# Norms that start earlier and other mixers in finer steps, in a hybrid decoder trunk

## The chip, the cores and the metric

The kernel runs on one core of a Trainium2 chip. The metric is the time of one execution on the device in microseconds (us); less is better. The engines of the core work side by side and wait for each other through semaphores: TensorE (PE) multiplies matrices, VectorE (DVE) and ScalarE (ACT) do elementwise work, GpSimd (POOL) does elementwise work that reads and writes SBUF alone, SyncE (SP) issues transfers; ACT issues transfers too. Each engine takes its own instructions in one fixed order.

## The reference, cut to what matters

```python
def rmsnorm(x, g):
    return x * lax.rsqrt(jnp.mean(x * x, axis=-1, keepdims=True) + 1e-6) * g
def run_layer(x, ...):                       # one layer, D_MODEL 1024
    z = rmsnorm(x, norm1_g) @ w_in           # (positions, 1024) @ (1024, 2432)
    zau, zav, zbu, zcx, zcb, zcc, zd = split(z)
    ya = chunk_gmlp(zau, zav, ...)           # A
    yb = s5_ssm(zbu, ...)                    # B: diagonal complex state space
    yc = short_conv(zcx, zcb, zcc, ...)      # C: y = zb * conv3(zc * zx)
    yd = rwkv7(zd, ...)                      # D: matrix state along the positions
    x = x + concat(ya, yb, yc, yd) @ w_out
    gate, up = split(rmsnorm(x, norm2_g) @ ffn_w_gu)
    return x + (silu(gate) * up) @ ffn_w_down     # FFN, inner width 2816
y_prompt = rmsnorm(run_layer(x_prompt, ...), norm_f_g)   # 2048 positions
y_sample = rmsnorm(run_layer(x_sample, ...), norm_f_g)   # 8 sequences, one position each
```

## The kernel before

The prompt is cut into four pieces of 512 positions (q = 0 to 3); activations lie transposed, features on partitions, positions in columns. The 8 sample columns ride with piece 1 in the mixers (520 columns) and with the last piece in the FFN. Every large product is made of an fp32r pass of the high parts (L281) and two bf16 passes with the low parts (L286), all in `mmg`. A weight tile is loaded into `raw` (three buffers in `wpool`), cast by ACT into `wh` (L240); the low part `wl` is made by DVE (L244) the first time and loaded back from memory (`lod`) afterwards.

The order of the work: first the 17 tiles `z` of piece 0 with the D mixer of that piece (until about 144 us); then `park(q)` for pieces 1, 2 and 3, which computes their z, scales it and puts it to memory (`zdr`), while the other mixers of piece 0 run; then for each piece the output projection (`outphase`), `norm2` and the FFN, beside which the mixers of the next piece run from the parked z; `final` is the last norm. On PE the order is written out: a `Strand` is a generator that yields numbers of ticks, a tick standing for one pass of 512 columns, and strands are taken up between the large products when their ticks have passed. The other engines take the order that the scheduler gives by priority (`hp`).

A norm is a `squares` and an `Rms`. `squares` squares the eight tiles of x (ACT), adds the first ones on POOL (L313) and the last ones on DVE (L317, L319); `rms` sums over partitions on PE (L338), takes a root and one Newton step (`newton`, on POOL unless it is given `V`, that is DVE; its last line is L296), spreads the result on PE (L354) and copies it out (ACT, L358). The gain g is put on x where x is converted to its high part `rh` (ACT) and low part `rl` (DVE, L384). So the products of a tile of z can run before the norm is known; the factor comes with the eviction (`zload` L790 for piece 0, `put_z` L757 for the others). In `norm1` x lies in tiles of the pool `zt_` (six) and the squares in tiles of `raw`:

```python
        def sq():
            return wpool.tile([P, TW], F32, tag="raw", bufs=3, name=nm("sq"))
        return h, Rms(squares(xk, w, sq, True), w, prio=MP, wait=64, gap=48)
```

`zrest` is the start of the mixers A to C: it loads z again, spreads two tiles into U5 (32 small copies, half on ACT, half on DVE, L834), makes the convolution (L850 to L866) and the statistics of v. POOL inverts small triangular matrices for the D mixer (L1259, L1261) and works off the constants of mixer B (`s5Q`, L520), of which ACT stores two halves (`s_q`, L676). In the FFN, L1445 to L1451 make silu(gate) * up (`gp`, `gr`, `ft`, `ah`, `al`) and L1464 adds the down projection into `xm`.

Of the kernel before, what the change touches and what calls it, by code (L numbers as in the profile page):

```python
# [65 lines left out]
def trunk(ctx: ExitStack, tc: tile.TileContext, I, O):  # L66
# [116 lines left out]
    def zwidth(q):  # L183
        return TW if q == SM else TP
# [117 lines left out]
    def squares(xk, w, new=at_, fast=False):  # L302
# [3 lines left out]
        for k in range(KT):  # L306
            if k == 0:
                act(acc[:, :w], xk(k), AF.Square)
                continue
            sq = new()  # L310
            act(sq[:, :w], xk(k), AF.Square)
            if not fast or k < 5:
                G.tensor_tensor(acc[:, :w], acc[:, :w], sq[:, :w], op=ALU.add)  # L313
            elif late is None:
                late = sq
            else:
                V.tensor_tensor(late[:, :w], late[:, :w], sq[:, :w], op=ALU.add)  # L317
# [85 lines left out]
    def norm1(q):  # L403

        w = zwidth(q)
        h = ring_tile(1)

        def xk(k):
            t = zt_("x")
            nc.sync.dma_start(t[:, :w], I["xq"][q, :, k, :w])  # L410
            put_gain(h, k, w, t[:, :w], "n1")
            return t[:, :w]

        def sq():
            return wpool.tile([P, TW], F32, tag="raw", bufs=3, name=nm("sq"))

        return h, Rms(squares(xk, w, sq, True), w, prio=MP, wait=64, gap=48)

# [3 lines left out]

    first = Rms(acc0, TP, wait=60, prio=18000)
    rs0 = acc0

# [80 lines left out]
    def s5_setup():  # L506
        with ExitStack() as c2:
# [183 lines left out]
            for pr in range(8):  # L691
# [4 lines left out]
                for g in range(2):  # L696
                    ps_ = slice(64 * g, 64 * g + 64)
                    for ri in range(2):
# [4 lines left out]
                        else:  # L703
                            act(cv[ps_, ri, g], bc[ps_, 3, pr], AF.Copy, scale=-1.0)
                            act(fv[ps_, ri, :, g], Ft[ps_, 1, pr], AF.Copy, scale=-1.0)
                yield 40 if pr == 0 else 20
                yield from ms_free()
# [76 lines left out]
    def zload(h, m, q, off=0):  # L784
        t = zt_()
        if q in parked:
            nc.sync.dma_start(t[:, off : off + zwidth(q)], zdr[q - 1, m, :, : zwidth(q)])
            return t
        for p_, (c0, n) in zip(ahead0.pop(0) if ahead0 else ztile(h, m, q), zblocks(q)):
            V.tensor_tensor(t[:, off + c0 : off + c0 + n], p_[:, :n], rs0[:, c0 : c0 + n], op=ALU.mult)  # L790
        return t

    def zrw(h, q):
        w = zwidth(q)
        zs = rw.tile([P, 7, TP], F32, tag="zs", name=nm("zs"))
        if q == 0:
            ahead0.extend(ztile(h, m, q) for m in range(4))
            first.done()
# [24 lines left out]
    def zrest(h, q, take):  # L823
# [4 lines left out]
        for j in range(2):  # L828
            zt = zload(h, 7 + j, q)
            for pr in range(4):  # L830
                src = zt[32 * pr : 32 * pr + 32, :TP].rearrange("p (c s) -> p c s", s=4)
                for s in range(4):
                    e = (S.copy, V.tensor_copy)[s % 2]
# [11 lines left out]
        ys = []  # L845
        for j in range(2):
            zx = zload(h, 9 + j, q)
            zz = zload(h, 11 + j, q, 2)
# [8 lines left out]
            if q == SM:  # L857
# [5 lines left out]
                nc.scalar.dma_start(O["cvs"][:, j, 0], cbuf[:, j, 1])  # L863
                nc.scalar.dma_start(O["cvs"][:, j, 1], zq)
            zb = zload(h, 13 + j, q)
            E.tensor_tensor(y[:, :w], y[:, :w], zb[:, :w], op=ALU.mult)  # L866
# [6 lines left out]
        vn = []  # L873
        for g, (b0, nb, rows) in enumerate(groups(q)):
            vt = zt_() if rows == P else vs
            n = 256 * nb
# [532 lines left out]
    def norm2(xm, q):  # L1409
# [7 lines left out]

        return h2, Rms(squares(xk, w, at_, True), w, V, prio=2 * RP, wait=30)

# [80 lines left out]
    def final(xm, q):  # L1500
# [8 lines left out]
        for k, t in enumerate(ts):  # L1509
            act(t[:, :w], xk(k), AF.Copy, scale=col("nf", k))  # L1510
        n = Rms(acc, w, prio=2 * RP, wait=40)

# [112 lines left out]
    m = Mix(0, h)  # L1625
    m.columns()
    m.start()
    with hp(MP):
        m.gm2 = m.rest()
        next(m.gm2)  # L1630
    for q in range(1, npiece):
        with hp(2 * RP):
            h, n1 = norm1(q)
        if q == 1:
# [4 lines left out]
    for q in range(npiece):  # L1639
        nx = Mix(q + 1) if q < last else None  # L1640
        if nx:
            nx.columns()
            nx.start(10)
        with hp(2 * RP):
# [144 lines left out]
```

## Time and profile before

| | |
|---|---|
| time, median of 3 runs | 2643.06 us (2640.42 to 2652.55) |
| the profiled execution's own time | 2647.65 us |
| its span in the profile | 2645.9 us |
| mean granted TensorE clock | 0.955 of full speed |
| busy: PE, DVE, ACT, POOL | 92%, 53%, 40%, 30% |

The profile is of one execution. Its span reaches from the first to the last instruction, its own time is 1.75 us longer. An engine's busy time is the time in which it had an instruction under way. The granted clock is given as a share of full speed (2.4 GHz); the lower of its two levels is 1.2 GHz.

### The profile page before, as it was taken

What the parts mean: (1) busy time and instruction counts of PE and PEld (TensorE: products, weight loads), DVE (VectorE), ACT (ScalarE), POOL (GpSimd) and SP (SyncE); (2) the same over time, 40 slices, a digit from 0 to 9 for tenths busy, and PEclk for the clock granted to TensorE, in tenths of its full rate; (3) what the DMA queues carried; (4) which work ended last, traced back from release to release, by engine and by line L of the source; (5) the groups of instructions that cost most, each with busy time, mean ns of one, the idle gap of its engine ahead of it and who ended that gap; (6) DMA issues with size and microseconds to landing.
All of it is one profiled execution on the core that took longest, in us unless ns stands there. A gap on an engine that the chain in (4) does not pass through costs nothing.

```text
span 2645.9 us, 39723 instructions
## 1 busy us (share of the span) xinstructions
PE 2422.5 (92%) x13857; PEld 1622.9 (61%) x14020; DVE 1414.7 (53%) x2790; ACT 1045.6 (40%) x2118; POOL 792.0 (30%) x1267
## 2 busy tenths in 40 slices
PE   7949979799979999999899999997999999999997
PEld 3638846555545556545466565554665558888886
DVE  6943233333788776656755554557555543333334
ACT  4542243433453333345533333544343435322223
POOL 6085116201263262032621711426235113100001
PEclk8978989899989999999999999998999999999999
DMA  5334546555444444464434544634444346444443
GB/s 170 112 115 145 174 133 192 162 155 181 120 126 126 134 138 129 131 185 141 147 120 125 156 128 138 214 110 146 128 135 145 109 141 203 130 134 134 137 138 99
DMA packets 285320, 375.86 MB, mean 142 GB/s; under 512 B 50968, under 2 KB 160576, under 8 KB 285120
## 3 DMA queue, kind: packets, MB, share of 16 engines
q1 hardware_dynamic: 239568, 323.19, 40.4%
q10 hardware_dynamic: 45552, 50.14, 5.4%
q8 instruction: 110, 1.80, 0.3%
q14 instruction: 90, 0.74, 0.1%
HBM read 318.89 MB, written 54.31 MB: 141 GB/s over the span
## 4 chain that ended last, share of the span: by engine, by line
PE 68%; POOL 10%; DVE 10%; issue 4%; DMA 4%; ACT 3%; ACTq 0%; SPq 0%; POOLq 0%; DVEq 0%
PE m L286 38%; PE m L281 21%; POOL BD L1261 3%; POOL inv L1259 3%; DMA z<-zdr 1%; PE x L1229 1%; DVE wl L244 1%; PE x L1305 1%; PE x L1296 1%; PE x L1285 1%; POOL rs L313 1%; POOL s5Q L520 1%; ACT wh L240 1%; DVE U L834 1%; PE ms L717 1%
## 5 line engine op out<-in xcount | busy, mean ns | idle before, releaser
L286 PE MATMUL m<-rl,wh 128*128 128x512 bf16 (+1 forms) x2758 | 847.4, 340 | 13.0 <-DVE rl L384 3.5
L286 PE MATMUL m<-rh,wl 128*128 128x512 bf16 (+1 forms) x2641 | 826.6, 347 | 0.1
L240 ACT CAST wh<-raw 128x512 fp32r<-128x512 f32 x744 | 451.7, 618 | 945.1 <-PE m L286 585.1
L281 PE MATMUL m<-rh,wh 128*128 128x512 f32 (+1 forms) x2760 | 652.5, 377 | 78.7 <-ACT wh L240 63.3
L286 PEld LDWEIGHTS <-wl 128*128 128x128 bf16 x3640 | 353.0, 100 | 350.9 <-issue 106.2
L281 PEld LDWEIGHTS m<-rh,wh 128*128 128x128 f32 x2760 | 455.2, 194 | 177.8 <-ACT wh L240 65.1
L286 PEld LDWEIGHTS <-wh 128*128 128x128 bf16 x3640 | 359.1, 99 | 237.1 <-issue 17.2
L1447 POOL TENSOR_TENSOR gr<-gp,rs 128x512 f32<-128x512 f32 (+1 forms) x110 | 124.9, 1144 | 749.3 <-DVE gp L1445 680.3
L1464 DVE TENSOR_TENSOR xm<-m,xm 128x512 f32<-128x512 f32 (+1 forms) x440 | 246.9, 581 | 128.4 <-PE m L286 119.0
L281 PE MATMUL m<-ah,wh 128*128 128x512 f32 (+1 forms) x880 | 250.8, 401 | 56.7 <-DVE gp L1445 16.0
L286 PE MATMUL m<-al,wh 128*128 128x512 bf16 (+1 forms) x880 | 275.9, 344 | 3.8 <-issue 1.3
L286 PE MATMUL m<-ah,wl 128*128 128x512 bf16 (+1 forms) x838 | 267.5, 351 | 0.7 <-DMA wl<-lod 0.7
L281 PEld LDWEIGHTS m<-ah,wh 128*128 128x128 f32 x880 | 149.2, 193 | 108.0 <-DVE xm L1464 19.1
L1259 POOL TENSOR_TENSOR inv<-BD 32x30 f32<-32x30 f32 (+14 forms) x240 | 132.3, 551 | 197.0 <-DMA BD<-dl 178.8
L244 DVE TENSOR_TENSOR wl<-raw,wh 128x512 bf16<-128x512 f32 x186 | 139.3, 757 | 59.9 <-ACT wh L240 56.4
L1445 DVE TENSOR_TENSOR gp<-m,rs 128x512 f32<-128x512 f32 (+1 forms) x110 | 62.1, 582 | 175.9 <-PE m L286 148.6
L1261 POOL TENSOR_TENSOR BD<-BD,inv 32x30 f32<-32x30 f32 (+14 forms) x240 | 148.4, 618 | 18.2
L1284 POOL TENSOR_SCALAR stl<-st,g 128x64 f32<-128x64 f32 x128 | 68.5, 549 | 276.6 <-DVE st L1299 256.3
L1448 DVE SCALAR_TENSOR_TENSOR ft<-ft,gr 128x512 f32<-128x512 f32 (+1 forms) x110 | 78.7, 730 | 83.6 <-POOL gr L1447 70.6
L1449 DVE SCALAR_TENSOR_TENSOR ft<-ft,m 128x512 f32<-128x512 f32 (+1 forms) x110 | 62.0, 580 | 99.8 <-PE m L286 98.8
L1451 DVE TENSOR_TENSOR al<-ft,ah 128x512 bf16<-128x512 f32 (+1 forms) x88 | 63.2, 718 | 35.9 <-ACT ah L1450 35.3
L757 DVE TENSOR_TENSOR zp<-m,rs 128x260 f32<-128x260 f32 (+1 forms) x68 | 35.8, 554 | 85.3 <-PE m L286 72.7
(378 smaller groups left out, 2677.3 us busy)
## 6 DMA issues: line engine op xcount, KB each, us to landing
raw<-in_wgu SPq DMA_DIRECT2D x352, 256.0 KB, 2.9
wl<-lod SPq DMA_DIRECT2D x558, 128.0 KB, 2.2
raw<-in_wd SPq DMA_DIRECT2D x176, 256.0 KB, 2.9
raw<-in_wz SPq DMA_DIRECT2D x136, 256.0 KB, 2.9
lod<-wl ACTq DMA_DIRECT2D x186, 128.0 KB, 3.2
raw<-in_wo SPq DMA_DIRECT2D x64, 256.0 KB, 3.3
zdr<-zp ACTq DMA_DIRECT2D x40, 256.0 KB, 2.9
z<-zdr SPq DMA_DIRECT2D x40, 256.0 KB, 3.7
```

What stands on the lines that cost most here:

```text
L240: S.copy(hi, raw)
L244: V.tensor_tensor(lo, raw, hi.bitcast(F32), op=ALU.subtract)
L281: T.matmul(p_[:, :n], lhsT=wh, rhs=xh[:, c0 : c0 + n], start=i == 0, stop=False)
L286: T.matmul(p_[:, :n], lhsT=a, rhs=b[:, c0 : c0 + n], start=False, stop=e and i == ends[id(ps)])
L1259: G.tensor_tensor(tv, xtv[:, 0:s, s : s + 1].to_broadcast([32, s, r]), xtv[:, s : s + 1, s + 1 :].to_broadcast([32, s, r]), op=ALU.mult)
L1261: G.tensor_tensor(xtv[:, 0:s, s + 1 :], xtv[:, 0:s, s + 1 :], tv, op=ALU.add)
L1284: G.tensor_scalar(stl[:, j], old[:, j], pvw[:, 8 * j + c, 32:33], None, op0=ALU.mult)
L1445: V.tensor_tensor(gp[:, c], pss[0][b][:, :n], rs[:, c], op=ALU.mult)
L1447: G.tensor_tensor(gr[:, c], gp[:, c], rs[:, c], op=ALU.mult)
L1448: V.scalar_tensor_tensor(tv, tv, 1.0, gr[:, c], op0=ALU.add, op1=ALU.mult)
L1451: V.tensor_tensor(al[:, :w], t[:, :w], ah[:, :w].bitcast(F32), op=ALU.subtract)
L1464: V.tensor_tensor(xm[m][:, c0 : c0 + n], p_[:, :n], xm[m][:, c0 : c0 + n], op=ALU.add)
```

## The change

The squares of the first norm are written over x, in x's own tile, and no longer into tiles of `raw`. Newton steps of this norm, for piece 0 too, go from POOL to DVE. Piece 1's `norm1` is called right after the set-up of piece 0's mixer, ahead of all the tiles of z, and its x lies in the two tiles `big0`, `big1` that held piece 0's x. Of piece 0's first four z tiles, two are copied from PSUM unscaled by ACT, and multiplied in place later. The strands get other numbers of ticks, and `zrest` yields 12 ticks at several places when the z was parked.

```diff
 def squares(xk, w, new=at_, fast=False):
+            x = xk(k)
             sq = new()
-            act(sq[:, :w], xk(k), AF.Square)
+            act(sq[:, :w], x, AF.Square)
...
 def norm1(q):
+        xs = []
+        big = [rw.tile([P, 4 * TW], F32, tag=f"big{i}", name=nm("x1")) for i in range(2)] if q == 1 else []
         def xk(k):
-            t = zt_("x")
+            t = big[k // 4][:, TW * (k % 4) : TW * (k % 4) + TW] if big else zt_("x")
             nc.sync.dma_start(t[:, :w], I["xq"][q, :, k, :w])
             put_gain(h, k, w, t[:, :w], "n1")
+            xs.append(t)
             return t[:, :w]
-        def sq():
-            return wpool.tile([P, TW], F32, tag="raw", bufs=3, name=nm("sq"))
-        return h, Rms(squares(xk, w, sq, True), w, prio=MP, wait=64, gap=48)
+        return h, Rms(squares(xk, w, lambda: xs[-1], True), w, V, prio=MP, wait=64, gap=48)
...
-    first = Rms(acc0, TP, wait=60, prio=18000)
+    first = Rms(acc0, TP, V, wait=60, prio=18000)
...
 def zload(h, m, q, off=0):
-        for p_, (c0, n) in zip(ahead0.pop(0) if ahead0 else ztile(h, m, q), zblocks(q)):
-            V.tensor_tensor(t[:, off + c0 : off + c0 + n], p_[:, :n], rs0[:, c0 : c0 + n], op=ALU.mult)
+        p_ = ahead0.pop(0) if ahead0 else ztile(h, m, q)[0]
+        if m < 2:
+            t, p_ = p_, p_[:, 1:]
+        else:
+            t = zt_()
+        V.tensor_tensor(t[:, off : off + TP], p_[:, :TP], rs0, op=ALU.mult)
...
 def zrw(h, q):
-            ahead0.extend(ztile(h, m, q) for m in range(4))
+            for m in range(4):
+                ahead0.append(ztile(h, m, q)[0])
+                if m < 2:
+                    t = zt_()
+                    S.copy(t[:, 1 : TP + 1], ahead0[m])
+                    ahead0[m] = t
...
 def zrest(h, q, take):        # the same two lines ahead of each of the 8 groups of U copies,
+                if q in parked:          # each of the 2 convolutions, each zb,
+                    yield 12             # and each group of v
...
-                yield 40 if pr == 0 else 20          # set-up of mixer B
+                yield 40 if pr == 0 else 28
-        return h2, Rms(squares(xk, w, at_, True), w, V, prio=2 * RP, wait=30)      # norm2
+        return h2, Rms(squares(xk, w, at_, True), w, V, prio=2 * RP, wait=48)
-        n = Rms(acc, w, prio=2 * RP, wait=40)        # final
+        n = Rms(acc, w, prio=2 * RP, wait=100)
...
     m.columns()
+    with hp(MP):
+        ahead = norm1(1)
     m.start()
...
-            h, n1 = norm1(q)
+            h, n1 = ahead if q == 1 else norm1(q)
...
-            nx.start(10)
+            nx.start(36)
```

On SP, where piece 2 begins, stood before (`wl` are low parts of weights, `x` the tiles of x, `raw` the weights of the first tiles of z):

```order
L242 DMA wl_3783<-lod 128x512
L242 DMA wl_3789<-lod 128x512
L410 DMA x_3669<-in_xq 128x512
L410 DMA x_3675<-in_xq 128x512
L410 DMA x_3682<-in_xq 128x512
L410 DMA x_3689<-in_xq 128x512
L410 DMA x_3696<-in_xq 128x512
L410 DMA x_3703<-in_xq 128x512
L242 DMA wl_3820<-lod 128x512
L410 DMA x_3709<-in_xq 128x512
L878 DMA vs<-zdr 8x256
L410 DMA x_3716<-in_xq 128x512
```

and after these rows the loads of `raw` for the first tiles. Now the first two `raw` tiles of the piece are loaded ahead of the rows below, and the next ones stand among the loads of x:

```order
L242 DMA wl_3765<-lod 128x512
L242 DMA wl_3771<-lod 128x512
L415 DMA x_3658<-in_xq 128x512
L415 DMA x_3663<-in_xq 128x512
L415 DMA x_3669<-in_xq 128x512
L415 DMA x_3675<-in_xq 128x512
L415 DMA x_3681<-in_xq 128x512
L415 DMA x_3687<-in_xq 128x512
L237 DMA raw_3799<-in_wz 128x512
L415 DMA x_3692<-in_xq 128x512
L237 DMA raw_3805<-in_wz 128x512
```

The loads of x have kept their place behind the last `wl`; the weights have come from behind them to ahead of and among them.

On ACT, in piece 1, the stores of s5Q's first half stood before between casts of weights (`wh`) and stores of z (`zdr`), far ahead of the copies for mixers B and D (`s5es`, `uv`):

```order
L758 DMA zdr<-zp_1764 128x520
L676 DMA s_q<-s5Q_2223 256x1x256
L240 CAST wh_1908<-raw_1906 128x512
L676 DMA s_q<-s5Q_2223 256x1x256
L240 CAST wh_1996<-raw_1994 128x512
```

Now they stand ten casts later, right behind the first `s5es` and ahead of a `uv`:

```order
L761 DMA zdr<-zp_2483 128x520
L716 COPY s5es_2512<-ms_2509 128x256
L717 DMA s_e<-s5es_2512 128x256
L679 DMA s_q<-s5Q_2212 256x1x256 x2
L704 COPY s5C_2331<-s5bc 64x16 x2
L188 ACTIVATE s5C_2331<-s5bc 64x16 x2
L724 DMA s_f<-s5Fz_2332 128x384
```

On DVE, in the FFN of piece 1, the copies into U5 stood before in one run between two steps of a gate (`gp`, `ft`, `al`):

```order
L1445 TENSOR_TENSOR gp_12102<-m_12039,rs_11423 128x512
L1448 SCALAR_TENSOR_TENSOR ft_12101<-ft_12101,gr_12103 128x512
L834 COPY U_216<-z_12127 32x128 x8
L834 COPY U_216<-z_12145 32x128 x8
L1449 SCALAR_TENSOR_TENSOR ft_12101<-ft_12101,m_12076 128x512
L850 TENSOR_TENSOR z_12165<-z_12165,z_12163 128x512
L853 TENSOR_SCALAR z_12170<-z_12165,c_pv 128x512
L855 SCALAR_TENSOR_TENSOR z_12170<-z_12165,c_pv,z_12170 128x512
L1451 TENSOR_TENSOR al_12105<-ft_12101,ah_12104 128x512
```

Now the first eight are cut in two, with steps of mixer D (`g`) behind them, and the other eight stand one gate later:

```order
L1466 TENSOR_TENSOR gp_12077<-m_11894,rs_11375 128x512
L1469 SCALAR_TENSOR_TENSOR ft_12076<-ft_12076,gr_12078 128x512
L849 COPY U_216<-z_12102 32x128 x6
L1197 MEMSET g_12257 128x528
L849 COPY U_216<-z_12102 32x128 x2
L1198 MEMSET g_12257 128x16
L1103 TENSOR_SCALAR g_12032<-g_12032 128x512
L1104 SCALAR_TENSOR_TENSOR g_12032<-g_12036,g_12032 128x512
L1470 SCALAR_TENSOR_TENSOR ft_12076<-ft_12076,m_12018 128x512
L1106 SCALAR_TENSOR_TENSOR g_12032<-g_12036,g_12032 128x512
L1472 TENSOR_TENSOR al_12080<-ft_12076,ah_12079 128x512
```

Between `ft` L1448 and L1449 sixteen copies have become eight copies and four other operations.

## Rows read from the trace of the kernel before

**Rows 1.** The page, section 1: busy time, share of the span, instructions.

```profile
PE 2422.5 (92%) x13857; PEld 1622.9 (61%) x14020; DVE 1414.7 (53%) x2790; ACT 1045.6 (40%) x2118; POOL 792.0 (30%) x1267
```

**Rows 2.** Busy time by stretch, then granted TensorE clock, DMA share, GB/s.

```profile
50.00:100.00 50.00, 49.48 (x219) 27.03 (x222) 47.88 (x114) 28.76 (x68) 3.64 (x10) 0.99 0.36 109
150.00:200.00 50.00, 21.99 (x145) 19.05 (x146) 20.31 (x26) 19.72 (x35) 44.87 (x91) 0.64 0.43 127
...
1300.00:1350.00 50.00, 37.24 (x177) 20.58 (x179) 41.32 (x81) 24.73 (x47) 23.75 (x51) 0.83 0.45 135
```

**Rows 3.** Timeline of PE: start, length, operation [idle before <-releaser].

```profile
37.49 1.99 PE L354 MATMUL ms<-c_ident,rt 128*128 128x128 f32 x8 [3.25 <-POOL rt L296]
46.24 3.78 PE L281 MATMUL m<-rh,wh 128*128 128x512 f32 x8 [6.75 <-DVE z L790]
...
111.27 0.49 PE L1229 MATMUL x<-RB,BD 128*128 128x128 f32 x2 [1.75 <-DVE BD L1223]
...
144.16 0.38 PE L286 MATMUL m<-rl,wh 128*128 128x512 bf16 x1
170.90 0.80 PE L281 MATMUL m<-rh,wh 128*128 128x260 f32 x2 [26.37 <-ACT wh L240]
...
192.14 2.08 PE L354 MATMUL ms<-c_ident,rt 128*128 128x128 f32 x8 [6.43 <-POOL rt L296]
...
241.72 3.02 PE L717 MATMUL ms<-s5C,s5R 128*128 128x32 f32 x16 [3.71 <-ACT s5es L713]
...
286.02 0.55 PE L1285 MATMUL x<-st,RB 128*128 128x64 f32 x4
```

**Rows 4.** Timeline of PE where pieces 2 and 3 begin.

```profile
348.28 0.27 PE L286 MATMUL m<-wl,rh 128*8 128x256 bf16 x1
366.49 0.80 PE L281 MATMUL m<-rh,wh 128*128 128x512 f32 x1 [17.95 <-ACT wh L240]
...
375.00 2.21 PE L281 MATMUL m<-rh,wh 128*128 128x512 f32 x8
...
499.28 0.27 PE L286 MATMUL m<-wl,rh 128*128 128x256 bf16 x1
518.58 0.79 PE L281 MATMUL m<-rh,wh 128*128 128x512 f32 x1 [19.03 <-ACT wh L240]
...
526.84 0.38 PE L286 MATMUL m<-rl,wh 128*128 128x512 bf16 x1
```

**Rows 5.** Timeline of SP, the queue of loads, at piece 2.

```profile
348.59 3.63 SPq L410 DMA_DIRECT2D x<-in_xq  x6
...
363.27 6.80 SPq L237 DMA_DIRECT2D raw<-in_wz  x7
```

**Rows 6.** Timeline of DVE at piece 2: conversions of x.

```profile
352.73 0.75 DVE L384 SCALAR_TENSOR_TENSOR rl<-x,c_pv,rh 128x512 bf16<-128x512 f32 x1 [6.98 <-ACT rh L188]
...
355.00 7.65 DVE L384 SCALAR_TENSOR_TENSOR rl<-x,c_pv,rh 128x512 bf16<-128x512 f32 x6 [0.38 <-ACT rh L188]
```

**Rows 7.** Timeline of POOL at piece 2: sums of squares.

```profile
354.43 6.34 POOL L313 TENSOR_TENSOR rs<-rs,sq 128x512 f32<-128x512 f32 x4 [10.68 <-ACT sq L188]
```

**Rows 8.** Timeline of POOL and of ACT's DMA issues: chain of s5Q.

```profile
181.04 0.26 POOL L520 TENSOR_TENSOR inv<-s5Q 128x4 f32<-128x4 f32 x1
...
239.39 1.19 ACTq L676 DMA_DIRECT2D s_q<-s5Q  x2
```

**Rows 9.** Groups of PE between 640 and 2200 us: down projections alone.

```profile
L281 PE MATMUL m<-ah,wh 128*128 128x512 f32 x528 | 180.2, 456 | 55.5 <-DVE gp L1445 16.0 <-DVE xm L1464 15.0 <-DVE ft L1449 10.6
```

**Rows 10.** Timeline of PE in the FFN of pieces 1 and 2.

```profile
1319.39 1.22 PE L281 MATMUL m<-ah,wh 128*128 128x512 f32 x2 [5.59 <-DVE gp L1445]
...
1739.11 1.84 PE L338 MATMUL ms<-c_ones,rs 128*128 128x1 f32 x8 [4.31 <-DVE rs L319]
...
1827.55 1.22 PE L281 MATMUL m<-ah,wh 128*128 128x512 f32 x2 [7.85 <-DVE gp L1445]
```

**Rows 11.** Timeline of DVE in the FFN of piece 1.

```profile
1295.61 8.94 DVE L834 COPY U<-z 32x128 f32<-32x128 f32 x16
```

More of the change, by code (lines that the diff above doesn't have):

```diff
@@ L421, in trunk @@
         h, acc0 = norm0()
-    first = Rms(acc0, TP, wait=60, prio=18000)
-    rs0 = acc0
+    first = Rms(acc0, TP, V, wait=60, prio=18000)
+    rs0 = acc0[:, :TP]
     glu = cload("glu", [P, 2, 256])
@@ L784, in zload @@
     def zload(h, m, q, off=0):
-        t = zt_()
         if q in parked:
+            t = zt_()
             nc.sync.dma_start(t[:, off : off + zwidth(q)], zdr[q - 1, m, :, : zwidth(q)])
             return t
-        for p_, (c0, n) in zip(ahead0.pop(0) if ahead0 else ztile(h, m, q), zblocks(q)):
-            V.tensor_tensor(t[:, off + c0 : off + c0 + n], p_[:, :n], rs0[:, c0 : c0 + n], op=ALU.mult)
+        p_ = ahead0.pop(0) if ahead0 else ztile(h, m, q)[0]
[4 more added lines that the diff above has]
+        V.tensor_tensor(t[:, off : off + TP], p_[:, :TP], rs0, op=ALU.mult)
         return t
@@ L796, in zrw @@
         if q == 0:
-            ahead0.extend(ztile(h, m, q) for m in range(4))
+            for m in range(4):
+                ahead0.append(ztile(h, m, q)[0])
+                if m < 2:
+                    t = zt_()
+                    S.copy(t[:, 1 : TP + 1], ahead0[m])
+                    ahead0[m] = t
             first.done()
@@ L846, in zrest @@
         for j in range(2):
+            if q in parked:
+                yield 12
             zx = zload(h, 9 + j, q)
@@ L864, in zrest @@
                 nc.scalar.dma_start(O["cvs"][:, j, 1], zq)
+            if q in parked:
+                yield 12
             zb = zload(h, 13 + j, q)
@@ L874, in zrest @@
         for g, (b0, nb, rows) in enumerate(groups(q)):
+            if q in parked:
+                yield 12
             vt = zt_() if rows == P else vs
```

## The prediction

> **What bounds the kernel now.** I read the page first: PE is busy for 2422.5 us [rows 1], while the profiled execution takes 2647.65. So the large products set the time, and a change that leaves them as they are can only win back the time in which PE stands still (its span of 2645.9 less 2422.5, 223 us in all) and the time in which it runs at the lower clock after one. The timeline of PE shows where it stands, and what released it. Three kinds of places matter here.
>
> First, the start of each piece. Piece 0's products end at 144.54 and piece 1's begin at 170.90; 6.43 us follow behind piece 1's Newton step on POOL [rows 3]. Pieces 2 and 3 begin with 17.95 and 19.03 us without work [rows 4]. The reader should look at SP there: it issues x at 348.59, but the weights `raw` only at 363.27, 14.7 us later [rows 5]. PE is not waiting for x. The squares occupy the three tiles of `raw`, and weights get no room until the squares are added.
>
> Second, the start of the kernel: waits of 3.25 and 6.75 us, released by POOL's Newton step and by the eviction of z on DVE [rows 3].
>
> Third, the FFN beside the mixers. Ahead of the down projections' products alone PE waits 55.5 us in pieces 0 to 2, mostly for `gp`, `xm` and `ft` on DVE [rows 9]; waits of 5.59, 7.85 and, ahead of norm2, 4.31 us are examples [rows 10]. In one such place DVE makes 16 copies into U5 for 8.94 us in one run, between two steps of a gate [rows 11].
>
> A wait costs more than itself: in 150 to 200 us the granted clock is 0.64, in 1300 to 1350 0.83, against 0.99 in 50 to 100 [rows 2]. Eight L281 products take 3.78 us behind the wait at 46.24 and 2.21 where PE has run for a while [rows 3, 4]. So 1.6 us per 8 such products is my price for the lower clock.
>
> **Pieces 2 and 3.** The weights of the first two half tiles can now be loaded and cast ahead of x. x itself does not come earlier, since in SP's new order it still stands behind the last `wl`. So PE can follow the conversion of x, tile by tile. In piece 2 the last product of before ends at 348.55, the first tile of z ends at 375.00: 26.4 us [rows 4]. The conversions on DVE run from 352.73 to 362.65 [rows 6]; one more k of three products, 1.1 us (a tile of eight takes 8.5 from 366.49), gives 363.8, which is 11.2 us earlier. Piece 3: 499.55 to 527.22 is 27.7 us; with the same conversions it needs some 16.3, so 11.4 less. I take 10.5 each, since x's last tile must now wait for its buffer until the square in it is added. The bounds: 7 (PE follows at the lower clock and keeps it into the second tile, two prices of 1.6) and 12 (nothing late).
>
> Here one rule speaks against the change. An `rl` takes 0.75 us alone; the last six take 7.65 us, 1.28 each, beside four additions on POOL of 1.59 each [rows 6, 7]. So each slows the other, but they overlap. The Trainium skill ("SBUF — State Buffer", Who interferes with whom) says that a DVE instruction with two SBUF inputs and a GpSimd instruction that reads SBUF exclude each other for a whole instruction. By that rule the conversions would end 8 x 0.75 + 6.34 = 12.3 us after 352.73, at 365.1, and each piece would win 8 and not 10.5. The trace has 362.65; I go by the trace.
>
> **Piece 1.** Its x is now loaded and converted at the very start, into the tiles of piece 0's x, and its norm lies among piece 0's products. In the section from 144.54 to 286.02 [rows 3], 26.37 and 6.43 us go, and the lower clock behind them: of 21.99 us of PE's work in 150 to 200, at 0.64 [rows 2], about 10 would be saved (all of it at half speed would be 11). What limits the section then is another chain: POOL inverts piece 0's matrices, starts s5Q at 181.04, and ACT issues its second store at 239.39 [rows 8]: 58 us, of which I count 26 for each half and 6 for the pause in which the first is stored. POOL loses four additions in front of it (4 x 1.59 = 6.3 at most [rows 7]), but the matrices' load stands behind two or three more transfers on SP, about one us each [rows 5], and POOL has other work between; so I put the halves' ends at 204 and 237 to 240. Without waits PE would reach what it reached at 286.02 already at 286.02 - 26.37 - 6.43 - 3.71 - 10 = 239.5. The first store now stands on ACT in front of `uv` copies and casts of weights that PE needs some 30 us before this point, at 206 to 210, just when the first half is done; the second store stands ahead of an `s5es` that PE needs here, just when the second half is done. I count 3 us of waits, 2.5 for the clock behind them and 1 to 2 for a later end of piece 0: 247, so 39 less; I take **38**. Bounds: 22 (all that hangs on the chain comes 12 us later, and the clock's price is paid again) and 46 (no wait on ACT).
>
> **The start.** The 6.75 and the clock behind it (1.6) go, since ACT copies two banks unscaled; of 3.25 half goes with POOL's Newton step. Against it: DVE is busy for 47.88 of 50 us between 50 and 100 [rows 2], and PE waits for it at 111.27 [rows 3]. The same DVE work must be done before the same products. POOL gets four more additions for piece 1 ahead of its chain (5 to 6 us), DVE the Newton steps and late sums of piece 1, ACT eight more conversions and squares; whatever PE wins at 40 it waits for at 111. I take 0. Bounds: 6 lost (the additions pass through whole), 8 won.
>
> **Finer steps.** Three pieces have the run of 8.94 us [rows 11]; cut in two and spread over two gates it should free half to all of it each time: 13 to 27 us. The longer waits of norm2 take away some of the 4.31 us [rows 10]; the rest are small. On the other side each of the new steps can meet a gate: I see new waits, and subtract some 8. I take 22 of the 55.5 [rows 9] and of the norms. Bounds: 45 won (two thirds of 55.5 and both norm2 waits), 15 lost. PE's own work is untouched: the last mixer's products still end well ahead of the last output projection, in the new order by 62 ticks less; the FFN of piece 2 covers that.
>
> **The sum.** 2647.65 - 0 - 38 - 10.5 - 10.5 - 22 = 2566.7 for the profiled execution. The median of the runs is 4.6 us below that execution, so **2562**. All bounds together give 2520 and 2628 by the median.
>
> **Rivals.**
> - *Handed back* (0.20): s5Q's chain and DVE set the ends. Piece 1 gives 22, the start loses 6, pieces 2 and 3 give 7 each, the finer steps nothing: 30 less, **2613**. For it: POOL is busy 44.87 of 50 us in 150 to 200 [rows 2], and ACT takes its instructions in order. Against it: pieces 2 and 3 have no such chain.
> - *All of it* (0.12): 8 + 46 + 12 + 12 + 37 is 115: **2528**. For it: the waits removed pull others with them, and the clock. Against it: 92% busy leaves little.
> - *Gates that wait* (0.03), the other side: the steps of `zrest` on DVE stand ahead of `gp` in every gate. There are 66 gates beside mixers; a wait of w in each costs 66 w. There the other terms, 59, are gone from 59/66 = 0.89 us on, more than one U copy (8.94/16 = 0.56 [rows 11]); with two copies, 1.12, it makes 2643 - 59 + 74 = **2658**. For it: DVE is busy for 41.32 of 50 us there [rows 2]. Against it: the rest of that is idle, and PE's wait ahead of `gp` alone is now 16.0 us for all 66 (528 products, eight a gate) [rows 9].
> - *It doesn't do what it says* (0.03): the room in `raw` is not what holds the weights, and piece 1's norm only trades places with s5Q's chain; then **2640**.
> - The skill's rule of the ports, as above, gives 2562 + 5 = **2567**; by these rows I give it 1 in 4 inside my forecast.
>
> **The numbers.** My forecast (0.62) has a range of its own from 2540 to 2590. Left out at 2528 and 2614 are the lower half of *all of it* and the two last cases, with part of *handed back*: 0.2. About 0.5%, 13 us, is what a measurement of this kernel can tell from no change; all but the last two cases lie below 2630, so faster 0.94, same 0.03, slower 0.03.
>
> **What would show it.** In the changed profile: PE's wait at pieces 2 and 3 is short and released by `rl` or `rh`, with their first tile of z done about 16 us after the last v; piece 1 follows piece 0 without a gap, with a wait of some us behind a store of `s_q`; a longer wait for `BD` near 111; DVE below 40 of 50 us in the stretches with the U copies, and less than 35 us ahead of the down projections. I am wrong if x's loads move too, if `s_q` holds ACT for over 10 us, or if the gates wait for the new steps.

## The result and the profile after

The changed kernel takes 2578.64 us in the median of four runs (2571.54 to 2580.82), against 2642.25 for the kernel before on the same chip. The ratio of the runs is 0.9747, with a 95% interval from 0.9715 to 0.9779: 2.5% faster, 64 us by the medians. 2562 had been forecast. The profiled execution took 2580.82 us, 66.8 less than that of before; it is these two traces that are compared place by place below.

The page of the changed kernel, section 1, busy time by engine:

```profile
PE 2409.8 (93%) x13856; PEld 1616.3 (63%) x14020; DVE 1420.9 (55%) x2810; ACT 1058.6 (41%) x2129; POOL 791.1 (31%) x1247
```

PE works for 12.7 us less than in [rows 1], with the same products, at a mean granted clock of 0.974 of full speed instead of 0.955: less of them run at the lower clock. The rest of the 67 us is time in which PE no longer stands still.

Where the time was won is read best as a lead. For an instruction that both kernels have, it is its time in the kernel before minus its time in the other one. The table gives it in us at nine places of the program: the end of piece 0's z; the last product of v of pieces 1, 2 and 3, where `park` of that piece ends; the first gate of the FFN of each piece (L1445 of before); the end of PE's work. The other columns are of the experiments below. Kernels that do not differ up to a place can still differ there by up to 4 us: at the last gate of piece 2 the lead is 72.2 in the changed kernel and 75.9 in a kernel that is equal to it up to there. So a difference of a few us counts only where further kernels with the same edit show it again.

```
place                time before  changed  own room  not early  coarse  no yields  room for x
end of z, piece 0        144.5      -5.4       0.2       3.5     -5.4      -5.1       -4.9
end of v, piece 1        348.5      35.3       0.9      15.0     32.9      37.2       36.6
end of v, piece 2        499.5      42.4       8.8      22.4     39.6      44.4       48.3
end of v, piece 3        638.2      50.2      17.4      32.7     47.8      51.6       59.3
first gate, piece 0      724.7      51.5      17.9      33.8     47.9      51.0       60.3
first gate, piece 1     1247.2      57.0      21.2      42.8     48.3      58.8       65.9
first gate, piece 2     1753.2      65.4      19.0      49.7     49.5      57.4       74.1
first gate, piece 3     2254.4      70.2      20.7      52.4     50.8      52.5       76.5
end of PE's work        2638.6      67.0      20.7      48.8     50.8      49.2       73.1
```

From one place to the next the changed kernel loses 5.4 us at the start, wins 40.7 in piece 1, 7.1 in piece 2, 7.8 in piece 3, and from there on 16.8: 20.0 up to the first gate of piece 3, less 3.2 in the last FFN.

**The start.** PE's timeline, as in [rows 3]:

```profile
56.63 3.49 PE L281 MATMUL m<-rh,wh 128*128 128x512 f32 x8 [4.52 <-DVE z L797]
...
90.52 2.07 PE L1128 MATMUL x<-g,c_blk 128*128 128x512 f32 x2 [4.24 <-ACT g L188]
...
149.57 0.38 PE L286 MATMUL m<-rl,wh 128*128 128x512 bf16 x1
149.59 0.58 PE L281 MATMUL m<-rh,wh 128*128 128x260 f32 x2
```

The wait of 6.75 us at 46.24 has become one of 4.52 at 56.63 and one of 4.24 at 90.52, and piece 0 ends at 149.95. Piece 1 follows without a gap: its first product starts at 149.59. What is late is DVE's first work on the constants of mixer B and, behind it, z:

```profile
51.99 0.29 DVE L633 TENSOR_TENSOR s5tmp<-t,s5bc 128x128 f32<-128x128 f32 x1 [1.75 <-POOL t L523]
52.20 1.30 DVE L797 TENSOR_TENSOR z<-z,rs 128x512 f32<-128x512 f32 x2
...
55.80 0.69 DVE L797 TENSOR_TENSOR z<-m,rs 128x512 f32<-128x512 f32 x1
```

The first of these rows, L633, stood at 43.06 before; now it is at 51.99, 8.9 us later, and the multiplications of z are queued behind it. It waits for POOL, which has four additions for piece 1 in front of its chain:

```profile
32.58 1.30 POOL L314 TENSOR_TENSOR rs<-rs,x 128x520 f32<-128x520 f32 x1
...
35.28 1.67 POOL L314 TENSOR_TENSOR rs<-rs,x 128x520 f32<-128x520 f32 x1
...
38.00 1.29 POOL L314 TENSOR_TENSOR rs<-rs,x 128x520 f32<-128x520 f32 x1
...
40.10 1.30 POOL L314 TENSOR_TENSOR rs<-rs,x 128x520 f32<-128x520 f32 x1
```

The additions take 5.6 us of the 8.9. The rest is in the chain's own small steps: up to the tile `s5s`, at 48.12, they take 30.6 us, against 27.0 in the kernel without the early norm below. DVE converts piece 1's x in that stretch; that this slows them is likely, but no run shows it by itself.

**Piece 1.** PE's waits of over one us between 150 and 313, and ACT's stores of s5Q:

```profile
188.88 1.54 PE L933 MATMUL ms<-wst,z 128*64 128x128 f32 x16 [3.11 <-DVE z L937]
...
213.38 0.69 PE L1317 MATMUL x<-uv,bt 128*128 128x64 f32 x4 [1.61 <-ACT uv L1312]
...
243.80 3.48 PE L720 MATMUL ms<-s5C,s5R 128*128 128x32 f32 x16 [3.77 <-ACT s5es L716]
```

```profile
210.94 1.25 ACTq L679 DMA_DIRECT2D s_q<-s5Q  x2
...
242.14 0.52 ACTq L679 DMA_DIRECT2D s_q<-s5Q  x1
```

The 26.37 and 6.43 us are gone. ACT does nothing for 5.60 us at the first store and 5.89 at the second. Behind the first store a `uv` copy comes 1.61 us late, behind the second an `s5es` 3.77; behind that one 16 products L720 take 3.48 us, where at full speed 16 took 1.97 (the row under *The stores of s5Q*). The wait of 3.11 for `z` on DVE is new.

**Piece 2.** PE, then DVE's conversions, SP's loads of x, ACT, and POOL's additions:

```profile
312.94 0.27 PE L286 MATMUL m<-wl,rh 128*8 128x256 bf16 x1
317.79 0.79 PE L281 MATMUL m<-rh,wh 128*128 128x512 f32 x1 [4.58 <-ACT rh L188]
...
323.12 0.58 PE L281 MATMUL m<-rh,wh 128*128 128x512 f32 x1
...
329.14 0.66 PE L281 MATMUL m<-rh,wh 128*128 128x512 f32 x1 [2.61 <-ACT rh L188]
...
330.12 3.42 PE L281 MATMUL m<-rh,wh 128*128 128x512 f32 x8
```

```profile
318.91 2.13 DVE L385 SCALAR_TENSOR_TENSOR rl<-x,c_pv,rh 128x512 bf16<-128x512 f32 x3 [0.38 <-ACT rh L188]
321.41 3.01 DVE L385 SCALAR_TENSOR_TENSOR rl<-x,c_pv,rh 128x512 bf16<-128x512 f32 x2 [0.37 <-ACT rh L188]
...
329.12 0.75 DVE L385 SCALAR_TENSOR_TENSOR rl<-x,c_pv,rh 128x512 bf16<-128x512 f32 x1 [0.33 <-ACT rh L188]
```

```profile
313.26 5.01 SPq L415 DMA_DIRECT2D x<-in_xq  x6
...
322.20 0.35 SPq L415 DMA_DIRECT2D x<-in_xq  x1
```

```profile
326.25 1.28 ACT L188 ACT_TABLE_LOAD   x1
327.54 0.41 ACT L188 ACTIVATE vs<-vs 8x256 f32<-8x256 f32 x1
...
328.37 0.72 ACT L188 ACTIVATE rh<-x,c_pv 128x512 fp32r<-128x512 f32 x1
```

```profile
320.84 6.38 POOL L314 TENSOR_TENSOR rs<-rs,x 128x512 f32<-128x512 f32 x4 [11.34 <-ACT x L188]
```

PE now starts 4.58 us behind the last v, where it had stood for 17.95 [rows 4], and follows the conversions. But the last tile of x is issued at 322.20 only, 4 us behind the block of six. Its buffer is one of the six of x, and holds a square until POOL has added it; the first of the four additions, which frees it, ends at 322.18. The tile lands at 325.65, and by then ACT has other work in its order: a table load and a `vs` of another mixer stand ahead of the last `rh` at 328.37. So PE waits 2.61 us, the first tile of z is done at about 330.7, 17.5 us behind the last v and not the 15.3 forecast, and the next eight L281 run at the lower clock, 3.42 us against 2.21 in [rows 4]. In piece 3 the last load waits for POOL's first addition too (it is issued at 467.88), but no table load follows.

Tile by tile, the changed kernel is 9.3 us ahead of the kernel before at the end of the first tile of z in piece 2 and 10.3 in piece 3, counted from the last v; at the end of the second tile 8.3 and 7.8 are left. Between the two PE does not wait; its products run at the lower clock.

**The FFN.** PE in the FFN of pieces 1 and 2 and at the last norm2, as in [rows 10]; DVE at the first of these places, as in [rows 11]; and the group of [rows 9]:

```profile
1254.55 1.22 PE L281 MATMUL m<-ah,wh 128*128 128x512 f32 x2 [7.73 <-DVE ft L1470]
...
1752.13 1.22 PE L281 MATMUL m<-ah,wh 128*128 128x512 f32 x2 [7.73 <-DVE ft L1470]
...
2182.09 1.44 PE L355 MATMUL ms<-c_ident,rt 128*128 128x128 f32 x8 [1.48 <-DVE rt L296]
...
2186.45 3.46 PE L281 MATMUL m<-rh,wh 128*128 128x260 f32 x15 [1.20 <-DVE gp L1466]
```

```profile
1247.50 0.69 DVE L1469 SCALAR_TENSOR_TENSOR ft<-ft,gr 128x512 f32<-128x512 f32 x1 [1.48 <-POOL gr L1468]
1248.23 5.55 DVE L849 COPY U<-z 32x128 f32<-32x128 f32 x8
1253.81 0.69 DVE L1470 SCALAR_TENSOR_TENSOR ft<-ft,m 128x512 f32<-128x512 f32 x1
```

```profile
L281 PE MATMUL m<-ah,wh 128*128 128x512 f32 x528 | 177.9, 454 | 38.8 <-DVE ft L1470 23.8 <-ACT ah L1471 9.8 <-DVE xm L1485 4.3
```

The waits ahead of the down projections fell from 55.5 to 38.8 us, and those for `gp` are no longer among the three longest kinds. The largest one left is the old one cut in half: eight copies into U5 still stand in one run of 5.55 us between two steps of a gate, and PE waits 7.73 for the `ft` behind them, in both pieces. In the kernel before such runs of 16 stand in the FFNs of pieces 1 and 2 alone. In the FFN of piece 0 its copies stand 8, 5 and 3 at a time, and there they are quick:

```profile
778.70 2.23 DVE L834 COPY U<-z 32x128 f32<-32x128 f32 x8
...
1297.59 0.58 POOL L1259 TENSOR_TENSOR inv<-BD 32x220 f32<-32x220 f32 x1
```

In both kernels a copy on DVE takes 0.26 to 0.28 us where POOL is idle, as here from 778.70 on. Where POOL works at the inverses, as it does beside the run of 16 of [rows 11], a copy takes 0.64 in the mean. At 0.27 the 16 copies would take 4.3 us and the eight 2.2, so more than half of the 8.94 and of the 5.55 us comes with what POOL does beside the copies. At the last norm2 there are new waits, 1.48 for DVE's Newton step and 1.20 for the first `gp`.

### The profile page after: what moved, and what is told of

It reads as the page before. It is cut to its first block, busy times and chain, and to the rows that moved or that the text cites. A ratio compares the mean times of both kernels' runs of the same rounds, so it can differ in the third digit from the quotient of the medians.

```text
span 2578.9 us, 39707 instructions
## 1 busy us (share of the span) xinstructions
PE 2409.8 (93%) x13856; PEld 1616.3 (63%) x14020; DVE 1420.9 (55%) x2810; ACT 1058.6 (41%) x2129; POOL 791.1 (31%) x1247
## 5 line engine op out<-in xcount | busy, mean ns | idle before, releaser
L281 PE MATMUL m<-rh,wh 128*128 128x512 f32 (+1 forms) x2760 | 645.8, 375 | 42.4 <-ACT rh L188 21.2
L281 PEld LDWEIGHTS m<-rh,wh 128*128 128x128 f32 x2760 | 451.5, 192 | 149.7 <-ACT rh L188 30.8
L281 PE MATMUL m<-ah,wh 128*128 128x512 f32 (+1 forms) x880 | 248.6, 399 | 40.0 <-DVE ft L1470 23.8
L1280 POOL TENSOR_TENSOR inv<-BD 32x30 f32<-32x30 f32 (+14 forms) x240 | 139.5, 581 | 233.9 <-DMA BD<-dl 215.7
L281 PEld LDWEIGHTS m<-ah,wh 128*128 128x128 f32 x880 | 149.7, 192 | 90.5 <-DVE ft L1470 26.3
L1282 POOL TENSOR_TENSOR BD<-BD,inv 32x30 f32<-32x30 f32 (+14 forms) x240 | 142.6, 594 | 18.2
```

Source lines behind the costliest of these rows:

```text
L281: T.matmul(p_[:, :n], lhsT=wh, rhs=xh[:, c0 : c0 + n], start=i == 0, stop=False)
L1280: G.tensor_tensor(tv, xtv[:, 0:s, s : s + 1].to_broadcast([32, s, r]), xtv[:, s : s + 1, s + 1 :].to_broadcast([32, s, r]), op=ALU.mult)
L1282: G.tensor_tensor(xtv[:, 0:s, s + 1 :], xtv[:, 0:s, s + 1 :], tv, op=ALU.add)
```

## The experiments

Twelve kernels were run, each timed in three rounds beside the kernel before on the same chip, and profiled once. Times of different chips are compared by their ratios to the kernel before; that of the changed kernel is 0.9747.

**Own room alone.** The kernel before, with the squares written over x:

```diff
-            act(sq[:, :w], xk(k), AF.Square)
+            x = xk(k); sq = new(); act(sq[:, :w], x, AF.Square)
...
-        return h, Rms(squares(xk, w, sq, True), w, prio=MP, wait=64, gap=48)
+        return h, Rms(squares(xk, w, lambda: xs[-1], True), w, prio=MP, wait=64, gap=48)
```

> The kernel before with one part of the change: the squares of the first norm in x's own tiles. Theory (each part wins in its own section and keeps it): pieces 2 and 3 win about 8 and 7 us as in the changed kernel, piece 1's wait of 26.4 us gets 5 to 10 us shorter, nothing else moves: 2620 us (2613 to 2626). Rival (the room in raw counts only together with the early norm and the finer order): under 8 us in all, above 2635.

Measured: 2627.82 us, ratio 0.9919 (0.9899 to 0.9940), about 21 us; the time is 2 us above the theory's range, on a chip on which the kernel before takes 2646.34. The column *own room* shows pieces 2 and 3 winning 7.9 and 8.6, as in the theory. Piece 1 wins 0.9 and not 5 to 10. PE there:

```profile
151.78 0.80 PE L281 MATMUL m<-rh,wh 128*128 128x260 f32 x2 [7.43 <-ACT rh L188]
...
163.49 0.80 PE L281 MATMUL m<-rh,wh 128*128 128x260 f32 x2 [4.54 <-ACT rh L188]
...
178.93 0.80 PE L281 MATMUL m<-rh,wh 128*128 128x260 f32 x2 [4.15 <-ACT rh L188]
...
195.24 2.08 PE L355 MATMUL ms<-c_ident,rt 128*128 128x128 f32 x8 [5.90 <-POOL rt L296]
```

PE starts 19 us earlier than before, and then waits for one `rh` after the other; the last comes at 178.93, and the norm at 195.24, where before it came at 192.14. The long wait was only cut into short ones. In piece 1 POOL is busy with the inverses, the additions stand between them, and x's buffers are free only after the additions: SP issues loads of x at 159.94, 161.98 and 169.53, each right behind the end of an addition (159.91, 161.96, 169.51). So own room alone does nothing for piece 1.

**The early norm taken out.** The changed kernel with

```diff
-    with hp(MP):
-        ahead = norm1(1)
...
-            h, n1 = ahead if q == 1 else norm1(q)
+            h, n1 = norm1(q)
```

and no `big` tiles for it.

> The changed kernel with piece 1's norm back in its old place. Theory: the early norm is worth about 40 us in piece 1 and costs 5 at the start; own room alone would still give piece 1 some 7, so this kernel loses 25 to 30 us: 2604 to 2610, and piece 0's products end at about 144.5 and not at 149.9. Rival (s5Q's chain on POOL sets the end of the section anyway): it loses under 15 us, below 2594. If the late end of piece 0 comes from the copied banks, it stays at 149 or later here.

Measured: 2602.07 us, ratio 0.9826 (0.9800 to 0.9852); it loses about 21 us, 18 by the lead at the end. Between the two ranges expected, nearer to the theory. Piece 0 ends 3.5 us earlier than before and not 5.4 later: the early norm costs the start 8.9 us, close to the 9.3 by which L633 is later with it (51.99 against 42.73). Without it piece 1 still wins 11.5, with it 40.7. So the early norm wins 29 and costs 9. That the 11.5 are not the 0.9 of own room alone is in part the Newton step on DVE, for which PE waits 2.43 us and not 5.90; the rest was not taken apart.

**Coarse steps again, and the yields alone.** One kernel has all numbers of ticks as before (20, 30, 40, 10 and no yields in `zrest`), the other only loses the yields:

```diff
-                if q in parked:
-                    yield 12          # all four places in zrest
```

> The changed kernel with all ticks as before: no yields in zrest, waits 20, 30, 40 and 10. Theory (by the lead of the changed kernel, which grows by 17 us from the first FFN on): 2594 to 2598. Rival (the waits among the FFNs are only moved, and the lead there comes from the earlier part): under 6 us lost, below 2585.

> The changed kernel without the yields of 12 in zrest, the other waits (28, 48, 100, 36) left as changed. Theory: of the 17 us of the finer steps the yields give the part inside the FFNs of pieces 1 and 2, 13 or so, and the waits of the norms give the rest: 2590 to 2594. Rival: the norms' waits and the later start of the next mixer give it all: 2576 to 2581.

Measured: coarse 2591.47 us, ratio 0.9787 (0.9764 to 0.9810), some 10.5 us lost; no yields 2593.85, 0.9799 (0.9780 to 0.9818), some 14 lost. The times alone can't tell the two from each other, and at the end the leads don't either (16.2 and 17.8 less than the changed kernel). What lies between does: from the first gate of piece 0 to that of piece 3 the changed kernel wins 18.7, coarse steps 2.9, and the longer waits without yields 1.5. Those waits win 8.5 between the FFNs of pieces 0 and 1 (50.3 at the last gate of piece 0) and lose 6.3 of it again by the first gate of piece 3. So without the yields the longer waits win nothing in sum, which is neither the theory's sum of two parts nor the rival. A kernel with the yields and the old waits was not run, so whether the waits add anything to the yields is not shown.

**Yields at the copies into U5 alone.** The three other places in `zrest` lose theirs.

> The changed kernel with the yields at the copies into U5 alone; those at the convolutions, the zb and v are taken out. Theory (the run of 16 copies on DVE between two steps of a gate was the cost): nearly all of the 14 to 18 us of the yields stays, 2578 to 2583. Rival (the work behind the copies, convolutions and v, crowds the gates as much): half is lost, 2585 to 2590.

Measured: 2586.44 us, ratio 0.9771 (0.9742 to 0.9800). Its lead grows by 11.1 between the first gates of pieces 0 and 3, against 18.7 and 1.5 with all and no yields: somewhat over half comes from the copies, the rest from convolutions and v. That is nearer to the rival, and the time lies in its range. The group of [rows 9] in this kernel and, below, without yields:

```profile
L281 PE MATMUL m<-ah,wh 128*128 128x512 f32 x528 | 178.2, 454 | 37.5 <-DVE ft L1464 22.6 <-ACT ah L1465 9.2 <-DVE xm L1479 3.4
```

```profile
L281 PE MATMUL m<-ah,wh 128*128 128x512 f32 x528 | 181.8, 459 | 48.9 <-DVE xm L1477 18.7 <-DVE gp L1458 11.8 <-ACT ah L1463 10.9
```

The waits for `gp` are gone with the copies' yields; those for `ft`, where the eight copies stand, have come. In sum they are no longer than in the changed kernel (37.5 against 38.8 us), so what the other yields win lies elsewhere in the FFNs; where was not pursued.

**The copied banks.** The changed kernel with the first four z evicted by DVE as before, and with all four copied by ACT instead of two:

```diff
-                if m < 2:          # none in the first kernel, in the second:
+                if m < 4:
```

> The changed kernel with the first four z tiles of piece 0 evicted and scaled by DVE, as before. Theory (the early conversions, sums and loads of piece 1's x cost about 9 us at the start, the copied banks and the Newton steps on DVE win 3 to 4 of them back): piece 0's products end at 151 to 154 instead of 149.9, the time is 1 to 4 us longer: 2580 to 2583. Rival (the copies themselves make the start late, as their later multiplication stands in a full DVE): they end at 147 or earlier and the time is 2 to 5 us shorter.

> The changed kernel with all four early banks copied unscaled by ACT. Theory (DVE is full from 45 to 120 us and sets the end of piece 0's products): PE's wait of 4.52 at 56.6 goes, but comes back at 90 to 120; the time stays within 2 us. Rival (the wait at 56.6 is worth itself): 4 us shorter.

Measured: none copied 2576.14 us, 0.9736 (0.9720 to 0.9752); four copied 2580.41, 0.9749 (0.9728 to 0.9770). Piece 0 ends at 151.7 in both, 1.8 later than with two, as the first theory had it, but the intervals all hold the changed kernel's ratio: the copies are worth no time that can be measured here. With none copied PE waits 9.31 and 6.06 us at 45.15 and 53.27, and the wait of 4.24 at 90.52 isn't there: what the copies save comes back. With four copied the wait of 4.52 is gone, and two of 2.69 and 3.64 for ACT's casts have come, which the copies stand among.

**The last norm2.** 30 ticks again for the piece without mixers beside it:

```diff
-        return h2, Rms(squares(xk, w, at_, True), w, V, prio=2 * RP, wait=48)
+        return h2, Rms(squares(xk, w, at_, True), w, V, prio=2 * RP, wait=30 if q == last else 48)
```

> The changed kernel with norm2 of the last piece, which has no mixers beside it, waiting 30 ticks as before and the others 48. Theory (48 ticks are as long as the products that can run ahead of that norm, so its Newton step is waited for): 2 to 5 us shorter, 2574 to 2577, and PE's waits of 1.48, 0.68 and 1.20 us near 2183 are gone. Rival (those waits come with either number): no change.

Measured: 2573.05 us, ratio 0.9726 (0.9707 to 0.9745). By the times alone the win is inside the uncertainty; by the trace it is there: the lead stays at 75.9 from the last gate of piece 2 to the end (75.7), where the changed kernel falls from 72.2 to 67.0. The two kernels below that have this edit too lose 0.2 there, and those with 48 ticks and all yields 5.1 to 5.3. Of the waits at that norm one row of over 0.4 us is left:

```profile
2178.59 0.39 PE L355 MATMUL ms<-c_ident,rt 128*128 128x8 f32 x2 [0.68 <-ACT rs L351]
```

**Room for x.** In pieces 2 and 3 the last three tiles of x go to tiles that only the FFN uses later:

```diff
-            t = big[k // 4][:, TW * (k % 4) : TW * (k % 4) + TW] if big else zt_("x")
+            t = big[k // 4][:, TW * (k % 4) : TW * (k % 4) + TW] if big else at_() if k > 4 else zt_("x")
```

> The changed kernel with the last three tiles of x of pieces 2 and 3 in tiles that only the FFN uses, so that their loads and conversions wait for no buffer. Theory (the first tile of z ends 17.4 us behind the last v and not 15.3 as forecast because the last tile of x comes late into its buffer, behind the sums on POOL): the wait of 2.6 us ahead of the last conversion goes, the pieces begin 2 to 5 us earlier each: 2569 to 2575. Rival (conversions at 1.2 us a tile set the end anyway): within 2 us.

Measured: 2571.76 us, ratio 0.9725 (0.9710 to 0.9740). Pieces 2 and 3 win 11.7 and 11.0 instead of 7.1 and 7.8; in the two kernels below that have this edit they win 11.4 and 10.9, 12.0 and 11.0. PE, DVE and POOL at piece 2:

```profile
318.17 0.80 PE L281 MATMUL m<-rh,wh 128*128 128x512 f32 x1 [6.31 <-ACT rh L188]
...
324.75 0.58 PE L281 MATMUL m<-rh,wh 128*128 128x512 f32 x1
...
326.81 2.21 PE L281 MATMUL m<-rh,wh 128*128 128x512 f32 x8
```

```profile
314.01 2.08 DVE L385 SCALAR_TENSOR_TENSOR rl<-at,c_pv,rh 128x512 bf16<-128x512 f32 x3 [3.01 <-ACT rh L188]
...
320.55 2.07 DVE L385 SCALAR_TENSOR_TENSOR rl<-x,c_pv,rh 128x512 bf16<-128x512 f32 x3
```

```profile
322.20 5.64 POOL L314 TENSOR_TENSOR rs<-rs,x 128x512 f32<-128x512 f32 x4 [13.22 <-ACT x L188]
```

Three tiles are converted by 316.1, before PE starts; no product waits behind the first one, the second tile of z starts at 326.81, and its eight L281 take 2.21 us: the clock has come back within the first tile and stays up. The edit does more than take the wait for the buffer away: three of the eight conversions now lie ahead of the others, and POOL's additions begin at 322.20, just as the last conversion ends (322.62), and no longer among them. So this run doesn't show how much of the win is the buffer, how much ACT's order and how much the additions out of the way. The time lies in the theory's range. By the whole program the 6 us lie at the edge of what the times can tell; at the two places themselves the leads are plain.

**The stores of s5Q from POOL.** `nc.scalar.dma_start(s5_q[...])` becomes `nc.gpsimd.dma_start(s5_q[...])`.

> The changed kernel with the two stores of s5Q issued from POOL, right behind the work that makes them, and no longer from ACT. Theory (ACT stands at these stores and holds up uv and s5es copies): PE's waits of 1.61 near 213 and 3.77 near 244 go, and the clock's price with them: 4 to 6 us shorter, 2573 to 2575. Rival (the uv and s5es copies are late by themselves, or POOL's issue makes the chain as much longer): within 2 us.

Measured: 2571.70 us, ratio 0.9714 (0.9688 to 0.9740). The lead at the end of v of piece 1 is 42.6, and 41.0 in the kernel with all three edits, instead of 33.2 to 37.9 in the kernels that have the early norm and the changed kernel's ticks there, but the stores on ACT: some 6 us in the mean. The waits of 1.61 and 3.77 are gone; at the place of the second stands

```profile
239.69 1.97 PE L720 MATMUL ms<-s5C,s5R 128*128 128x32 f32 x16 [0.89 <-ACT s5es L716]
```

**Both, and all three.** The edits of the last norm2 and of x's room together, and with s5Q's stores from POOL.

> The changed kernel with both of the edits that won: the last three tiles of x of pieces 2 and 3 in tiles of the FFN, and 30 ticks for the last norm2. Theory (two separate places): both wins add, 10 to 12 us below the changed kernel, 2565 to 2570. Rival (what one wins the other gives back): 5 to 6 us.

> The two edits that won and the stores of s5Q from POOL together. Theory: if the stores win alone, 14 to 17 us below the changed kernel, 2562 to 2566. Rival: as the two edits alone.

Measured: both 2569.76 us, ratio 0.9708 (0.9684 to 0.9733); all three 2565.07, ratio 0.9685 (0.9659 to 0.9711), an interval that lies below that of the changed kernel. Both times lie in the theories' ranges. At their own places the three edits had won 5.0 (the last norm2), 7.8 (pieces 2 and 3) and some 6 (piece 1). At the end of PE's work the two kernels are 12.1 and 15.2 ahead of the changed one: the wins add, as far as leads that scatter by up to 4 us can tell.

## Why the prediction was right, and where its sum was off

The forecast of 81 us stands against 67, with the time inside the likeliest case's own range. The mechanisms of pieces 1, 2 and 3 were right; three of the four terms were too high. In the order of the program (start, piece 1, pieces 2 and 3, finer steps) the terms are off by -5.4, +2.7, -6.1 and -5.2 us, so the time is not in its range because large errors cancelled. By the prediction's terms:

- **Pieces 2 and 3**, 10.5 each: 7.1 and 7.8. The mechanism was right: PE follows the conversions tile by tile, as own room alone shows too. Two things were mis-sized. The step that let x's last tile wait for its buffer counted under 1 us: in piece 2 the load waited for POOL's first addition, and then the conversion behind a table load on ACT, so that the first tile of z was done 17.5 us behind the last v and not 15.3. And the clock's price, which the sum kept for its lower bound, was paid: of 9.3 and 10.3 us won at the first tile 8.3 and 7.8 were left after the second. With room for x the pieces win 11.7 and 11.0, about the count without the wait (11.2 and 11.4), but there three tiles are converted ahead, which that count did not have. The rule of the ports had given 8, close to what was measured; that is luck, since in piece 2 DVE had nothing but a copy of 0.42 us to do in the 3 us before the last conversion. Its sum also took the additions at 6.34 us, which has their waiting in it; with 1.30 for one alone it is 8 x 0.75 + 4 x 1.30 = 11.2 us, until 363.9, which makes 9 us and not 8. So rule and forecast lay too close for these times to tell them apart. What the rows show of the rule is below.
- **Piece 1**, 38: 40.7. The chain of s5Q ended 2 us later than the 237 to 240 forecast (its second store is issued at 242.14) and its first half 7 later than 204 (210.94), and ACT did stand there ahead of `uv` and `s5es`. Some 6 us hung on it, as the stores from POOL show; 5.5 had been counted, with the clock. The wait of 3.11 for `z` had not been.
- **The start**, 0: 5.4 lost, inside its bound of 6. This is the one term with a wrong balance. The bound was that POOL's four additions pass through; they passed through whole, since L633 on DVE stands behind POOL and z behind L633, and POOL's own chain took 3.6 us longer, which the bound had at nothing. The early norm costs 8.9, banks and Newton steps return 3.5. That the copied banks win the 6.75 us is refuted: they win no time that can be measured, and their wait comes back, though at 90 and not at 111 as forecast.
- **Finer steps**, 22: 16.8. The sum counted three runs of 8.94 us; the kernel before has two, and where the third was counted, in the FFN of piece 0, 1.3 us were lost (51.5 to 50.2). In the FFNs of pieces 1 and 2 7.7 and 6.8 were won, which is within the half to all of 8.94 that was forecast for each; at the norms ahead of these two FFNs 6.8 and 0.7. The last norm2 lost 5.2, where the kernels with 30 ticks lose 0.2; I had not forecast this, though the last piece has no mixers to fill 48 ticks.

Of the rivals, *handed back* holds for the kernel with own room alone, in piece 1, where a wait of 26 us was cut up and not shortened, and for the copied banks at the start. Gates did not wait for the new steps in sum, and DVE's copies remain the largest wait in the FFN. Of the signs, DVE is below 40 of 50 us in the stretches with the copies (38.61 in 1250 to 1300) and `s_q` holds ACT for less than 10 us, as forecast; the longer wait for `BD` near 111 did not come, and 38.8 us ahead of the down projections are more than the 35 named. Why the longer waits without yields win 8.5 us and lose them again was not pursued.

## What to carry to other kernels

A long wait that is released by one thing can hide the next one right behind it: to know what its removal is worth, follow the data that comes last (here x's last tile, its buffer, its place in ACT's order), not the engine that waits. A store that waits for a slow chain holds up all that stands behind it on the queue it is issued from; here it cost some 6 us more on ACT than on POOL, the engine that ends the chain. And compare kernels by leads at the same instructions: they put a win in its section, which times that scatter by some tenths of a per cent can't, and kernels that are equal up to a place show how far the leads can be trusted.

## What the runs showed of the hardware

A conversion on DVE with two inputs in SBUF (`rl`) took 0.75 us alone and 0.69 in a row of three with POOL idle; beside POOL's additions two of them took 3.01, 1.5 each. An addition took 1.30 where DVE stood idle, and 1.6 beside the conversions. In [rows 6, 7] four conversions and the four additions lie beside each other, from 354.43 to 361.32: 6.9 us, where one behind the other they would take 4 x 0.75 + 4 x 1.30 = 8.2. The Trainium skill ("SBUF — State Buffer", Who interferes with whom) has one of them wait for the whole of the other's instruction; the rows agree with it in direction, not in full.

The small copies into U5 on DVE, which have one input, slow down beside POOL too: 0.26 to 0.28 us with POOL idle, 0.64 in the mean beside its inverses in the kernel before.

The lower clock came behind each of the long waits, and how long it stayed differs. Behind 6.31 us the kernel with room for x ran the first products of the tile at 0.77 to 0.99 us for one L281, and from 324.05 on at 0.60 and 0.58, so the second tile's eight took 2.21; the granted clock was 0.65 of full speed in 317 to 327 and 1.00 in 326 to 332. In the changed kernel the clock had come back too behind 4.58 us (0.58 at 323.12), but fell again with the wait of 2.61, and the second tile's eight took 3.42, at 0.77 in 330 to 336.
